# Chained products in PSUM, weight pieces kept from the first half, and operands fetched a stage ahead

## The chip, the cores and the metric

The kernel runs on one core of a Trainium2 chip. The metric is the device time of one execution in microseconds. The median of three runs is 3549.64 us (3546.86 to 3550.24).

## The reference

One layer of an encoder on 2048 tokens of width 1024, fp32: a token mixer (a chunked mLSTM beside an RWKV-7 recurrence), cross-attention on 256 memory rows, and a gated feed-forward part with a causal convolution of width 3; each adds to x behind an RMS norm, and a last norm follows. The part that matters here is the last:

```python
def conv_glu_ffn(h, w_up, conv_w, conv_b, w_down):
    u = h @ w_up
    gate, val = u[..., :D_FF], u[..., D_FF:]
    gate = causal_dwconv(gate, conv_w, conv_b)
    return (jax.nn.silu(gate) * val) @ w_down
...
        h = rmsnorm(x, norm_ffn[l])
        x = x + conv_glu_ffn(h, f_up[l], f_conv_w[l], f_conv_b[l], f_down[l])
    return rmsnorm(x, norm_final)
```

D_FF is 2816, in 22 tiles of 128 (`f` below). The kernel holds everything transposed, features on the partitions and tokens along the free axis.

## The kernel before

Every matmul operand is split into a rounded part hi and a rest lo, and a product is the three matmuls hi·hi, hi·lo and lo·hi, of 128x128 weights against 512 tokens. A split is a cast on ScalarE and a subtraction on VectorE or GpSimd (`resplit`, L1330 and L1331).

The mixer takes the first 1335 us and is not touched. All that follows is one block whose instructions a scheduler has put in order beforehand, engine by engine, by a model of their costs; on the chip each engine works through its queue in that order. SP issues all DMAs, in order too. The block goes over two halves of 1024 tokens; a half has two blocks of 512 (`NB`).

For each half: cross-attention (`attention`, with `out_proj` for the second block, and `attn_out`, which also makes the seven operands that the up-projection needs), then `ffn_up`, then `ffn_down`. The output projection of the next half's first block stands ahead of the last of the four groups of `ffn_down` (`ahead`).

`ffn_up` takes the gate and the value columns of one f as a 2x2 block matrix (input halves against gate and value), and the two token blocks as the other side, and forms the result by seven products instead of eight: weights a11, a12, a22 and the sums s1 to s4 against the operands 11, t1, t3, t2, 21, 22, t4. Each product is 12 matmuls, so 84 per f. The raw columns come by `load_raw` (two buffers, `wraw`); s1 to s4 are added in fp32 (L1417 to L1420) and the seven pieces are split, in both halves anew. Four PSUM tiles X, Z, W, Y take the products; p1, p5 and p7 are copied to SBUF (L1436), and VectorE and GpSimd add them (u2 at L1451, p7+p5 at L1452, c21 at L1479, p7+u2 at L1480). `gate(b)` multiplies by the row scale bc3, runs the convolution (Identity on ScalarE, two taps at L1467), the tanh (L1470), L1471 and a multiplication by bc3 on GpSimd (L1472). L1482 makes the result and L1483 stores it to `act_dram`.

`ffn_down` goes through four groups (token block b, output half dh). Each takes 22 steps of 12 matmuls (L1502 to L1504). A step loads 256 KB of weights into `wdr` (6 buffers, shared with other temporaries) and splits them into `wd`; in groups with dh 0 it loads and splits the activations of that f as well. At a group's end the four sums are added to x2 (L1508), and behind dh 1 the last norm follows.

## Time and profile before

| | us |
|---|---|
| median of three runs | 3549.64 |
| the profiled execution | 3561.95 |
| its span | 3560.2 |
| TensorE busy in it | 3281.8 |
| VectorE busy | 2298.4 |
| GpSimd busy | 1581.8 |
| ScalarE busy | 1355.2 |

The granted TensorE clock is 0.963 over the span. Up-projections lie at 1717 to 2197 us and 2780 to 3269 us, the first down-projection begins at 2216 us (the next half's output projection is in it), the second lies at 3285 to 3544 us. A line of a timeline has the start, the duration, the engine, the line of the program, the operation with output and inputs, its shape, and in brackets how long the engine was idle just before and what released it. Matmuls overlap, so their pace is the distance of their starts. Releasers are inferred.

### The profile page before, as it was taken

Reading aid. Unit: us, or ns where it says so; the run is one execution under the profiler, and the core shown is the slowest. Engines: PE = TensorE matmul, PEld = TensorE weight load, DVE = VectorE, ACT = ScalarE, POOL = GpSimd, SP = SyncE. Lnnn points to the kernel's source line nnn. Section 1 sums busy time; section 2 is a strip of 40 time slices with the busy share of each in tenths; the row PEclk is TensorE's granted clock in tenths of the full one; section 3 lists DMA queues with packets and bytes.
Section 4 is the critical chain, followed back from the end, with each engine's and each line's share of the span. In section 5 each row is a group of like instructions: output and inputs, shape, how many; then the busy total and the mean of one; then the engine's idle time right before and its main releaser. Section 6 shows DMA issues by size and latency. Waiting matters only on the chain. (4 is left out here: it accounts for less than half of the span.)

```text
span 3560.2 us, 48232 instructions
## 1 busy us (share of the span) xinstructions
PE 3281.8 (92%) x16860; PEld 2654.7 (75%) x16860; DVE 2298.4 (65%) x4104; ACT 1355.2 (38%) x2703; POOL 1581.8 (44%) x1486
## 2 busy tenths in 40 slices
PE   6999999999999988999799997997999799997998
PEld 5777778788778777787677775876887677775876
DVE  5787777777777764343798999222233799899221
ACT  5345433533434345332333334333232333334322
POOL 5332121211211123431788887554231688886543
PEclk9999999999999999999899998998999899998999
DMA  6555444544544448657222224444557222223442
GB/s 215 199 176 174 141 141 138 169 130 128 157 127 137 129 151 266 231 173 248 80 74 71 74 72 167 157 158 143 171 172 240 83 76 72 74 74 144 155 151 83
DMA packets 279283, 509.28 MB, mean 143 GB/s; under 512 B 85504, under 2 KB 117376, under 8 KB 279040
## 3 DMA queue, kind: packets, MB, share of 16 engines
q1 hardware_dynamic: 274816, 504.10, 43.1%
q8 instruction: 133, 2.18, 0.3%
q10 hardware_dynamic: 4224, 2.10, 0.2%
q14 instruction: 110, 0.90, 0.1%
HBM read 396.96 MB, written 109.12 MB: 142 GB/s over the span
## 5 line engine op out<-in xcount | busy, mean ns | idle before, releaser
L147 PE MATMUL pd<-hA,whl 128*128 128x512 f32 x2976 | 815.5, 411 | 14.7 <-ACT whl L121 6.6
L147 PEld LDWEIGHTS pd<-hA,whl 128*128 128x128 f32 x2976 | 535.1, 191 | 119.2 <-ACT whl L121 8.3
L1430 PE MATMUL pd<-h,ws 128*128 128x512 f32 x704 | 293.3, 417 | 59.0 <-ACT ws L1330 59.0
L1502 PE MATMUL dps<-act,wd 128*128 128x512 f32 x704 | 281.8, 400 | 66.7 <-ACT wd L1330 66.7
L1331 POOL TENSOR_TENSOR wd<-wdr,wd 128x512 fp32r<-128x512 f32 x176 | 235.6, 1355 | 194.6 <-ACT wd L1330 192.4
L124 POOL TENSOR_TENSOR whl<-wraw,whl 128x512 fp32r<-128x512 f32 x137 | 187.0, 1375 | 253.4 <-ACT whl L121 245.3
L1431 PE MATMUL pd<-h,ws 128*128 128x512 f32 x704 | 284.8, 405 | 0.0
L1503 PE MATMUL dps<-act,wd 128*128 128x512 f32 x704 | 280.7, 399 | 0.0
L1432 PE MATMUL pd<-h,ws 128*128 128x512 f32 x704 | 271.2, 406 | 0.0
L1504 PE MATMUL dps<-act,wd 128*128 128x512 f32 x704 | 268.4, 392 | 1.1 <-POOL wd L1331 1.1
L1430 PEld LDWEIGHTS pd<-h,ws 128*128 128x128 f32 x704 | 137.7, 196 | 117.8 <-ACT ws L1330 94.9
L1331 POOL TENSOR_TENSOR a<-wraw,a 128x512 fp32r<-128x512 f32 x132 | 210.4, 1594 | 2.2 <-ACT a L1330 2.2
L1502 PEld LDWEIGHTS dps<-act,wd 128*128 128x128 f32 x704 | 135.7, 193 | 98.0 <-ACT wd L1330 69.7
L1430 PE MATMUL pd<-h,a 128*128 128x512 f32 x528 | 206.7, 391 | 0.0
L1431 PE MATMUL pd<-h,a 128*128 128x512 f32 x528 | 206.0, 390 | 0.0
L1432 PE MATMUL pd<-h,a 128*128 128x512 f32 x528 | 205.8, 390 | 0.0
L1331 POOL TENSOR_TENSOR ws<-sr,ws 128x512 fp32r<-128x512 f32 x88 | 146.9, 1670 | 88.4 <-ACT ws L1330 88.4
L1219 POOL TENSOR_TENSOR sq<-sq 128x512 f32<-128x512 f32 x56 | 76.0, 1357 | 231.6 <-ACT sq L1216 230.2
L1432 PEld LDWEIGHTS pd<-h,ws 128*128 128x128 f32 x704 | 137.1, 195 | 42.3 <-POOL ws L1331 11.3
L1330 ACT CAST wd<-wdr 128x512 fp32r<-128x512 f32 x176 | 108.2, 619 | 158.4 <-PE dps L1504 101.4
L1472 POOL TENSOR_TENSOR fu<-fu,bcs 128x512 f32<-128x512 f32 x88 | 142.2, 1616 | 54.4 <-DVE fu L1471 54.4
L1508 DVE TENSOR_TENSOR x<-dps,x 128x512 f32<-128x512 f32 x32 | 21.7, 690 | 214.0 <-PE dps L1504 214.0
(992 smaller groups left out, 8054.6 us busy)
## 6 DMA issues: line engine op xcount, KB each, us to landing
whl<-w_split SPq DMA_DIRECT2D x186, 512.0 KB
wraw<-f_up SPq DMA_DIRECT2D x88, 512.0 KB
wdr<-f_down SPq DMA_DIRECT2D x176, 256.0 KB
wqk<-qk_dram SPq DMA_DIRECT2D x64, 512.0 KB
wvo<-vo_dram SPq DMA_DIRECT2D x64, 512.0 KB
w_split<-whl SPq DMA_DIRECT2D x62, 512.0 KB
act_dram<-fu SPq DMA_DIRECT2D x88, 256.0 KB
act<-act_dram SPq DMA_DIRECT2D x88, 256.0 KB
```

The source lines that it names most:

```text
L124: (nc.vector if dve else nc.gpsimd).tensor_tensor(t_[:, 1], r_, t_[:, 0].bitcast(F32), ALU.subtract)
L147: nc.tensor.matmul(out_, lhsT, rhs, **kw)
L1219: (nc.vector if fast else nc.gpsimd).tensor_tensor(acc, acc, sq, ALU.add)
L1330: nc.scalar.copy(t_[:, 0], raw)
L1331: eng.tensor_tensor(t_[:, 1], raw, t_[:, 0].bitcast(F32), ALU.subtract)
L1430: nc.tensor.matmul(ps, w[:, 0, k, :], B[b][k][:, 0, :], start=(k == 0 and not more), stop=False, skip_group_check=True)
L1431: nc.tensor.matmul(ps, w[:, 0, k, :], B[b][k][:, 1, :], start=False, stop=False, skip_group_check=True)
L1432: nc.tensor.matmul(ps, w[:, 1, k, :], B[b][k][:, 0, :], start=False, stop=(k == H - 1), skip_group_check=True)
L1472: nc.gpsimd.tensor_tensor(u, u, bc3[b], ALU.mult)
L1502: nc.tensor.matmul(pss[i], hi[:, i, :], a[:, 0, :], start=(f == 0), stop=False)
L1503: nc.tensor.matmul(pss[i], hi[:, i, :], a[:, 1, :], start=False, stop=False)
L1504: nc.tensor.matmul(pss[i], lo[:, i, :], a[:, 0, :], start=False, stop=(f == NFF - 1))
```

## The change

Four things change, all of them in the second block.

The products are accumulated in PSUM in chains: X takes a11, s2, s3 and a22 in turn and is copied out after each but the last (p1, u2, u3), Z takes s1 and then s4, and R takes a12. There are three PSUM tiles per f, and the additions u2, c21, p7+p5 and p7+u2 are replaced by an addition R+p1 in gate(0) and u3+p5 on GpSimd. gate(0) now adds from PSUM and multiplies by bc3 in SBUF, as gate(1) did. ScalarE copies four tiles per f.

In the first half each split piece is stored to `ws_dram` (512 KB each). The second half loads the seven pieces of an f from there and splits none of them.

The down-projection's operands are fetched ahead: in the last f of `ffn_up` the first four weights and the first seven activations, before each group's drain the first four weights of the next group, and activations of the second block during the group before it. `wdr` moves to another pool of four buffers.

In `attn_out` the sum of squares stands ahead of the splits, for the second block on VectorE; the row scale of the second block is made after the products of f = 0.

```diff
+    ws_dram = dram.tile([NFF, 7, P, 2, KT // 2, P], F32, name="ws_dram")
...
+            acc = sum_sq(acc, x, d, o == 1)
...
-            acc = sum_sq(acc, x, d)
...
+    def up_weights(hf, f):
 
         H = KT // 2
-        whl = lambda name: wpool.tile([P, 2, H, P], FR, tag="whl", name=name, bufs=WB)
-        bc3 = None
+        pcs = {}
+
+        def piece(i, name):
+            pool = name[0] == "a"
+            pcs[name] = wpool.tile([P, 2, H, P], FR, tag="whl", name="wa", bufs=WB) if pool else KQ((P, 2, H, P), "ws")
+            if hf:
+                nc.sync.dma_start(pcs[name].bitcast(F32), ws_dram[f, i])
+            return pcs[name]
...
+        rg, rv = load_raw(t_in["f_up"][f]), load_raw(t_in["f_up"][NFF + f])
+        g1, g2, v1, v2 = rg[:, :H], rg[:, H:], rv[:, :H], rv[:, H:]
+        s1r, s2r, s3r, s4r = [t_[:, u] for t_ in [K4((P, 2, H, P), "sr", F32) for _ in range(2)] for u in range(2)]
+        raws = dict(a11=g1, a12=g2, a22=v2, s1=s1r, s2=s2r, s3=s3r, s4=s4r)
+        for i, name in enumerate(order):
+            t_ = piece(i, name)
+            if name == "s1":
+                nc.gpsimd.tensor_tensor(s1r, v1, v2, ALU.add)
+            elif name == "s2":
+                nc.vector.tensor_tensor(s2r, s1r, g1, ALU.subtract)
+            elif name == "s3":
+                nc.vector.tensor_tensor(s3r, v1, g1, ALU.subtract)
+            elif name == "s4":
+                nc.gpsimd.tensor_tensor(s4r, g2, s2r, ALU.subtract)
+            resplit(t_, nc.vector if name in ("s2", "s3") else nc.gpsimd, raws[name])
+            if S > HALF:
+                nc.sync.dma_start(ws_dram[f, i], t_.bitcast(F32))
+        return pcs
...
+            last = f == NFF - 1
+            X, Z, R = [PD(name="pd") for _ in range(3)]
+            prod(X, "a11", "11")
             p1 = kept(X, "p1")
-            prod(Z, s1, "t1")
+            prod(Z, "s1", "t1")
             p5 = kept(Z, "p5")
-            prod(W, s3, "t3")
-            p7 = kept(W, "p7")
-            prod(Y, s2, "t2")
-            if bc3 is None:
-                norm_bc(st[NB - 1])
-                bc3 = [s_["bc3"] for s_ in st]
-            u2 = T(name="u2")
-            nc.vector.tensor_tensor(u2, Y, p1, ALU.add)
-            nc.gpsimd.tensor_tensor(p7, p7, p5, ALU.add)
+            if last:
+                early(range(3))
+            prod(X, "s2", "t2", True)
+            u2 = kept(X, "u2")
+            prod(R, "a12", "21")
+            if last:
+                early(range(3, 7))
...
-                if b == 0:
-                    nc.vector.tensor_tensor(gt_[:, 2:], X, bc3[b], ALU.mult)
-                else:
-                    nc.vector.tensor_tensor(gt_[:, 2:], Z, u2, ALU.add)
-                    nc.vector.tensor_tensor(gt_[:, 2:], gt_[:, 2:], bc3[b], ALU.mult)
+                nc.vector.tensor_tensor(gt_[:, 2:], (R, Z)[b], (p1, u2)[b], ALU.add)
+                nc.vector.tensor_tensor(gt_[:, 2:], gt_[:, 2:], st[b]["bc3"], ALU.mult)
...
-            prod(X, a12, "21", True)
-            gate(0)
-            prod(Z, s4, "22", True)
+                nc.gpsimd.tensor_tensor(u, u, st[b]["bc3"], ALU.mult)
+
+            if f:
+                gate(0)
+            prod(X, "s3", "t3", True)
+            u3 = kept(X, "u3")
+            nc.gpsimd.tensor_tensor(u3, u3, p5, ALU.add)
+            prod(Z, "s4", "22", True)
+            if f == 0:
+                prod(X, "a22", "t4", True)
+                norm_bc(st[NB - 1])
+                gate(0)
             gate(1)
-            prod(W, a22, "t4", True)
-            nc.vector.tensor_tensor(c21, W, u2, ALU.add)
-            nc.vector.tensor_tensor(p7, p7, u2, ALU.add)
-            for b, c in enumerate((c21, p7)):
+            if f:
+                prod(X, "a22", "t4", True)
+            for b, c in enumerate((X, u3)):
...
+    class Down:
+
+        def __init__(self, hf):
+            self.hf, self.have = hf, {}
+
+        def act(self, b, f):
+            if (b, f) not in self.have:
+                a = self.have[b, f] = K4((P, 2, TB), "act")
+                nc.sync.dma_start(a[:, 1].bitcast(F32), act_dram[self.hf, f, b])
+                resplit(a, nc.vector)
+            return self.have[b, f]
+
+        def w(self, b, dh, f):
+            H = KT // 2
+            if (b, dh, f) not in self.have:
+                w, raw = KQ((P, 2, H, P), "wd"), TQ((P, H, P), "wdr")
+                nc.sync.dma_start(raw, t_in["f_down"][f][:, dh * H:(dh + 1) * H])
+                resplit(w, nc.gpsimd, raw)
+                self.have[b, dh, f] = w
+            return self.have[b, dh, f]
+
+        def early(self, fs):
+            for f in fs:
+                if f < 4:
+                    self.w(0, 0, f)
+                self.act(0, f)
...
+                if dh == 1 and b + 1 < NB and 6 <= f < 12:
+                    D.act(b + 1, f - 6)
...
+            if not lastg:
+                for f in range(4):
+                    D.w(*groups[n + 1], f)
```

VectorE in the up-projection of half 0, before, from the late part of one f to the start of the next (pd is a PSUM tile, sr an unsplit sum, ws a split piece, bcs the row scale, fu the gate):

```order
2743 L1464 TENSOR_TENSOR gt__18790<-gt__18790,bcs_17781 128x512
2744 L1331 TENSOR_TENSOR ws_18828<-sr_18831,ws_18828 128x512
2745 L1331 TENSOR_TENSOR ws_18829<-sr_18832,ws_18829 128x512
2746 L1467 SCALAR_TENSOR_TENSOR fu_18753<-gt__18790,vec_68,fu_18753 128x512 x2
2747 L1479 TENSOR_TENSOR c21_18754<-pd_18694,u2_18750 128x512
2748 L1482 SCALAR_TENSOR_TENSOR fu_18753<-fu_18753,c21_18754 128x512
2749 L1471 SCALAR_TENSOR_TENSOR fu_18753<-fth_18798,fu_18753 128x512
2750 L1482 SCALAR_TENSOR_TENSOR fu_18753<-fu_18753,p7_18736 128x512
2751 L1451 TENSOR_TENSOR u2_18909<-pd_18854,p1_18867 128x512
2752 L1480 TENSOR_TENSOR p7_18895<-p7_18895,u2_18909 128x512
2753 L1461 TENSOR_TENSOR gt__18926<-pd_18851,bcs_17312 128x512
```

L1479, L1451 and L1480 in these rows are the additions that go, and L1461 at the end is gate(0)'s multiplication out of PSUM.

The same queue in the changed program, from the two splits of one f over gate(1) to gate(0) of the next:

```order
2682 L1332 TENSOR_TENSOR ws_18212<-sr_18201,ws_18212 128x512
2683 L1332 TENSOR_TENSOR ws_18221<-sr_18202,ws_18221 128x512
2684 L1474 TENSOR_TENSOR gt__18169<-pd_18073,u2_18115 128x512
2685 L1475 TENSOR_TENSOR gt__18169<-gt__18169,bcs_17828 128x512
2686 L1478 SCALAR_TENSOR_TENSOR fu_18129<-gt__18169,vec_68,fu_18129 128x512 x2
2687 L1482 SCALAR_TENSOR_TENSOR fu_18129<-fth_18177,fu_18129 128x512
2688 L1499 SCALAR_TENSOR_TENSOR fu_18129<-fu_18129,u3_18154 128x512
2689 L1474 TENSOR_TENSOR gt__18293<-pd_18237,p1_18250 128x512
2690 L1475 TENSOR_TENSOR gt__18293<-gt__18293,bcs_17313 128x512
2691 L1430 TENSOR_TENSOR sr_18365<-wraw_18362,wraw_18360 128x512
2692 L1478 SCALAR_TENSOR_TENSOR fu_18292<-gt__18293,vec_68,fu_18292 128x512
2693 L1499 SCALAR_TENSOR_TENSOR fu_18129<-fu_18129,pd_18072 128x512
```

gate(1) now stands as one run, with the final of u3 right behind it, and gate(0) of the next f begins with an addition and a multiplication; the final that reads the PSUM tile (pd) stands between the two taps of the next f.

GpSimd in the changed program at the same f:

```order
626 L1483 TENSOR_TENSOR fu_18129<-fu_18129,bcs_17313 128x512
627 L1332 TENSOR_TENSOR ws_18226<-sr_18202,ws_18226 128x512
628 L1479 COPY fcar_15470<-gt__18169 128x2
629 L1332 TENSOR_TENSOR wa_18366<-wraw_18360,wa_18366 128x512
630 L1473 COPY gt__18293<-fcar_15470 128x2
631 L1483 TENSOR_TENSOR fu_18129<-fu_18129,bcs_17828 128x512
632 L1489 TENSOR_TENSOR u3_18154<-u3_18154,p5_18101 128x512
633 L1332 TENSOR_TENSOR wa_18380<-wraw_18360,wa_18380 128x512
```

The addition of p5 to u3 stands directly behind gate(1)'s multiplication; before, the addition of p7 and p5 stood behind it in the same way, but the row that read it was not the next one of VectorE.

In the second half of the changed program one f has ten such rows on VectorE (four for each gate and two finals); no difference and no split is left.

SP before the last group of half 0, before (wdr are down weights, wraw and x the output projection's operands):

```order
1203 L1262 DMA x_22864<-xT 128x512
1204 L96 DMA wraw_23947<-w_out 128x1024
1205 L1270 DMA x1_dram_15462<-x_22864 128x512
1206 L1262 DMA x_22907<-xT 128x512
1207 L1270 DMA x1_dram_15462<-x_22907 128x512
1208 L1262 DMA x_22950<-xT 128x512
1209 L1270 DMA x1_dram_15462<-x_22950 128x512
1210 L1518 DMA wdr_22990<-f_down 128x512
1211 L1518 DMA wdr_23007<-f_down 128x512
```

Here the weight loads of the last group follow the output projection's last store.

The same place in the changed program:

```order
1361 L1518 DMA wdr_22700<-f_down 128x512
1362 L1518 DMA wdr_23147<-f_down 128x512
1363 L1518 DMA wdr_23164<-f_down 128x512
1364 L1518 DMA wdr_23181<-f_down 128x512
1365 L1518 DMA wdr_23198<-f_down 128x512
1366 L1518 DMA wdr_23215<-f_down 128x512
1367 L1518 DMA wdr_23232<-f_down 128x512
1368 L1263 DMA x_22759<-xT 128x512
1369 L1518 DMA wdr_23249<-f_down 128x512
1370 L1271 DMA x1_dram_15462<-x_22759 128x512
```

Six of the last group's weight loads now stand ahead of the output projection's first load of x and a seventh ahead of its first store; the four before them (the last is row 1361) stand there as well.

## Rows read from the trace of the kernel before

**Rows 1.** Windows of three stretches: busy time by engine, granted clock, DMA share.

```profile
core 0: us, PE busy (x) PEld busy (x) DVE busy (x) ACT busy (x) POOL busy (x), PEclk, DMA share, GB/s
1350.00:1400.00 50.00, 45.92 (x303) 40.28 (x302) 24.65 (x38) 27.85 (x52) 18.76 (x15) 0.97 0.92 294
1745.60:2196.00 450.40, 424.36 (x1779) 334.66 (x1779) 407.15 (x380) 169.76 (x294) 367.88 (x294) 0.98 0.22 75
3269.10:3285.30 16.20, 0.01 (x1) 0.01 (x1) 16.20 (x26) 13.66 (x25) 4.75 (x3) 0.58 1.03 388
```

**Rows 2.** Timeline of TensorE: start, duration, operation, idle before and its releaser.

```profile
1679.48 0.39 PE L176 MATMUL pd<-pt,wvo 128*128 128x512 f32 x1
...
1692.86 0.39 PE L175 MATMUL pd<-pt,wvo 128*128 128x512 f32 x1
...
1717.88 1.87 PE L1225 MATMUL ssps<-ones,sq 128*128 128x1 f32 x8 [10.13 <-POOL sq L1219]
...
2216.36 0.80 PE L1502 MATMUL dps<-act,wd 128*128 128x512 f32 x1 [18.82 <-ACT wd L1330]
...
2476.90 0.80 PE L1502 MATMUL dps<-act,wd 128*128 128x512 f32 x1 [20.93 <-ACT wd L1330]
...
2789.43 1.87 PE L1225 MATMUL ssps<-ones,sq 128*128 128x1 f32 x8 [9.26 <-POOL sq L1219]
...
2796.55 1.86 PE L1234 MATMUL bcB<-ident,rstd 128*128 128x128 f32 x7 [5.25 <-POOL rstd L183]
...
3285.29 0.80 PE L1502 MATMUL dps<-act,wd 128*128 128x512 f32 x1 [16.20 <-ACT wd L1330]
...
3544.11 0.39 PE L1504 MATMUL dps<-act,wd 128*128 128x512 f32 x1
```

**Rows 3.** All operations of line L1461, two of half 0: durations, start.

```profile
L1461 DVE TENSOR_TENSOR gt__17972<-pd,bcs x1: 677/677/677, 1766.6 to 1766.6; 128x512 f32<-128x512 f32 x1
...
L1461 DVE TENSOR_TENSOR gt__20834<-pd,bcs x1: 676/676/676, 2153.8 to 2153.8; 128x512 f32<-128x512 f32 x1
```

**Rows 4.** Timeline of VectorE, one f of the up-projection.

```profile
1895.63 0.68 DVE L1461 TENSOR_TENSOR gt__18926<-pd,bcs 128x512 f32<-128x512 f32 x1
1896.23 0.68 DVE L1418 TENSOR_TENSOR sr<-wraw 128x512 f32<-128x512 f32 x1
1897.26 2.28 DVE L1467 SCALAR_TENSOR_TENSOR fu<-gt__18926,vec,fu 128x512 f32<-128x512 f32 x2 [0.35 <-POOL fcar L1468]
...
1901.26 1.78 DVE L1464 TENSOR_TENSOR gt__18949<-gt__18949,bcs 128x512 f32<-128x512 f32 x1
...
1913.63 1.76 DVE L1482 SCALAR_TENSOR_TENSOR fu<-fu,p 128x512 f32<-128x512 f32 x1 [1.41 <-POOL fu L1472]
1915.31 0.68 DVE L1451 TENSOR_TENSOR u<-pd,p 128x512 f32<-128x512 f32 x1
1916.09 1.14 DVE L1480 TENSOR_TENSOR p<-p,u 128x512 f32<-128x512 f32 x1
1917.15 0.68 DVE L1461 TENSOR_TENSOR gt__19085<-pd,bcs 128x512 f32<-128x512 f32 x1
```

**Rows 5.** Waits of TensorE, 1350 to 3560 us: total, times, longest.

```profile
PE pd L1430 <- ACT ws L1330: 59.0, 42, 2.1
```

**Rows 6.** Timeline of GpSimd in the same f.

```profile
1912.30 1.29 POOL L1472 TENSOR_TENSOR fu<-fu,bcs 128x512 f32<-128x512 f32 x1 [0.63 <-DVE fu L1471]
1913.55 1.29 POOL L1452 TENSOR_TENSOR p<-p,p 128x512 f32<-128x512 f32 x1
```

**Rows 7.** Timeline of VectorE, first f of half 0.

```profile
1744.95 0.69 DVE L1451 TENSOR_TENSOR u<-pd,p 128x512 f32<-128x512 f32 x1 [7.61 <-PE pd L1432]
...
1757.01 2.45 DVE L1467 SCALAR_TENSOR_TENSOR fu<-gt__17836,vec,fu 128x512 f32<-128x512 f32 x2 [0.95 <-ACT fu L1465]
```

**Rows 8.** Waits of TensorE, 2230 to 2470 us.

```profile
PE dps L1502 <- ACT wd L1330: 6.7, 2, 4.7
```

**Rows 9.** DMA issues on SP before the last group of half 0.

```profile
2472.84 0.33 SPq L1270 DMA_DIRECT2D x_dram<-x  x1
2473.22 6.92 SPq L1518 DMA_DIRECT2D wdr<-f_down  x6
```

More of the change, by code (lines that the diff above doesn't have):

```diff
@@ new lines, in up_weights @@
+        pcs = {}
[5 more added lines that the diff above has]
+            return pcs[name]
+        order = ("a11", "s1", "s2", "a12", "s3", "s4", "a22")
+        if hf:
+            for i, name in enumerate(order):
+                piece(i, name)
+            return pcs
@@ new lines, in ffn_down, with step @@
+            lastg = n == len(groups) - 1
+            if dh == 0:
+                xs, acc = [], None
+            if lastg:
+                ahead()
+            tail = 4 if lastg else 0
+            pss = [PD(name="dps") for _ in range(H)]
+            def step(f, i):
+                w, a = D.w(b, dh, f), D.act(b, f)
+                nc.tensor.matmul(pss[i], w[:, 0, i, :], a[:, 0, :], start=(f == 0), stop=False)
+                nc.tensor.matmul(pss[i], w[:, 0, i, :], a[:, 1, :], start=False, stop=False)
+                nc.tensor.matmul(pss[i], w[:, 1, i, :], a[:, 0, :], start=False, stop=(f == NFF - 1))
@@ new lines, in ffn_down @@
+            for f in range(NFF):
+                D.w(b, dh, f)
+                D.act(b, f)
+                if f < NFF - tail:
+                    for i in range(H):
+                        step(f, i)
+                if f in (NFF - 4, NFF - 2):
+                    xx = K4((P, 2, TB), "x2", F32)
+                    for u in range(2):
+                        nc.sync.dma_start(xx[:, u], x2_dram[len(xs), :, ts_])
+                        xs.append(xx[:, u])
+                if dh == 1 and b + 1 < NB and 6 <= f < 12:
+                    D.act(b + 1, f - 6)
@@ new lines, in ffn_down @@
+            if not lastg:
+                for f in range(4):
+                    D.w(*groups[n + 1], f)
+            for i in range(H):
+                for f in range(NFF - tail, NFF):
+                    step(f, i)
+                x = xs[dh * H + i]
+                nc.vector.tensor_tensor(x, pss[i], x, ALU.add)
+                acc = sum_sq(acc, x, dh * H + i, True)
+            if dh:
+                bc = bcast_sbuf(acc)
+                for d in range(KT):
+                    nc.vector.scalar_tensor_tensor(xs[d], xs[d], V("norm_final", d), bc, ALU.mult, ALU.mult)
+                    nc.sync.dma_start(out[d * P:(d + 1) * P, ts_], xs[d])
```

89 lines of the change are left out of this document (15 added, 74 removed).

## Prediction

> **What bounds the kernel now.** I read the windows of the stages first, then the waits of TensorE, then the timeline of one f on VectorE and GpSimd, last TensorE's own rows where it stood still longest. In the windows the reader is to see that the gated up-projection is not a transfer problem: the DMA engines are busy 0.22 of it, while VectorE is busy 407 of 450 us; in another stage they carried 294 GB/s at a share of 0.92, so about 320 GB/s is theirs to give [rows 1]. TensorE is busy too, but its rows are modelled ends; its pace is read from spacing: 60 rows from 1679.48 to 1692.86 are 59 steps, 0.2268 us each [rows 2]. The 84 matmuls of one f would take 19.05 us at that pace. One f takes (2153.8 - 1766.6)/18 = 21.51 us [rows 3]. So 2.46 us per f are lost, 22 times in each half.
>
> Who takes them stands in VectorE's timeline [rows 4]: from one L1461 to the next (1895.63 to 1917.15) it is idle only 0.35 + 1.41 us. It works through its queue in order for 19.76 us and waits in it for 1.76; TensorE's 59.0 us behind "ACT ws" [rows 5] are the same delay seen one step on. Why 18 operations of about 0.60 us (issue to issue beside a source in PSUM, 1895.63 to 1896.23) last 19.76 us is in the same rows: those with both inputs in SBUF take 1.7 to 1.8 us when GpSimd works beside them, while those that read PSUM stay at 0.68. GpSimd has ten large operations per f, 1.25 us each when nothing is beside them (1912.30 to 1913.55 [rows 6]).
>
> The rest of the loss is at seams [rows 2]: TensorE waits 10.13 us for the sum of squares before half 0's first up-product, 18.82 between up and down, 20.93 at the last group behind the next half's output projection; in half 1 9.26 and 5.25, then 16.20.
>
> **The change, part by part.**
>
> *Matmuls.* Their number stays, 84 per f and 12 per step of the down-projection. Chaining sums in PSUM takes nothing from TensorE.
>
> *VectorE in half 0.* Three additions go: u2 (0.60 to the next start, or 0.78 as 1915.31 to 1916.09 has it), c21 (as a PSUM reader 0.60) and p7+u2 (1.06). The final of X reads PSUM instead of SBUF, about 0.3 less. gate(0) had one operation (L1461, 0.60); it now has an addition from PSUM (0.60) and a multiplication in SBUF, 0.60 alone or 1.71 beside GpSimd (1901.26 [rows 4] to the next start). Together -2.6 and +0.6 to +1.7: work falls from 19.76 to between 17.8 and 18.9. But waits grow, since the new order gives less to do between a request and its answer: both of gate(1)'s and half of gate(0)'s wait for the Identity of ScalarE stand open (0.95 as in [rows 7], and 0.33 of it), that for tanh costs about 0.7, and the final of u3 now waits for two GpSimd operations in a row, fu*bc3 and then u3+=p5 behind it: 1.41 as now, plus 1.25, is 2.66. In all 4.6 us. A plain sum gives 22.4 to 23.5 per f. Against it stands that GpSimd moves on during those 2.9 new idle us, and each of its operations that runs then lengthens none of VectorE's. The floor is what cannot overlap: ten operations of GpSimd at 1.25 and 13 of VectorE with both inputs in SBUF at 0.60 are 20.3 us. I take 21.8, near the middle of 20.3 and 23.5 and nearest to the row of now: 21 periods cost 6 us (from 25 gained to 42 lost). ScalarE's fourth copy out of PSUM (0.58 by its kind) lies in its idle time.
>
> The Trainium skill ("SBUF — State Buffer", section "SBUF: two separate sides") says that VectorE with two SBUF inputs and GpSimd share a pair of ports as an exclusive lock: whichever starts first holds it for its whole instruction. The rows of 0.68 against 1.7 to 1.8 agree. By that rule the moved multiplication, no longer read from PSUM, costs up to 1.1 us per f, 23 us over 21 periods, and by the other reading, in which it costs 0.60 whatever stands beside it, 23 us less; 21.8 lies between.
>
> *Stores in half 0.* Seven pieces of 512 KB per f besides two raw loads of 512 and two activation stores of 256: 5.24 MB, at 320 GB/s 16.4 us of 21.8. They are hidden if the queue keeps the loads early enough: on SP the second raw load stands behind the store of s3, which waits for VectorE's subtraction, and by the order some 11 us remain before its first reader. If that cover goes, each f pays what is missing of the 11.
>
> *Seams of half 0.* Attention to up: gate(0) of f=0 needs no bc3 of block 1 and VectorE no longer stands 7.61 us [rows 7] for the product s2·t2: 7.5 gained. The statistics' product keeps its place directly before the broadcast, so its wait stays (bounds 0 to 15). Up to down: the first pieces of the down weights are split early, but TensorE's last products wait for the last gate, whose VectorE steps are queued behind the early splits of activations, and the load of the seventh piece stands on SP behind the last activation store: of 18.82 I count 4 (0 to 15). Between the first groups 6.7 us of waiting [rows 8] are lost, and four weights are ready before the drain: 6. Last group: now SP issues its six weight loads at 2473.22, behind the last store of the output projection, 3.7 us before the first matmul that had waited 20.93 [rows 2, 9]; in the new order eleven weights are loaded and seven split before that projection: 21 (10 to 21). Half 0 in all: 7.5 - 6 + 4 + 6 + 21 = 32.5.
>
> *Half 1.* It loads the seven pieces and splits nothing: VectorE keeps 12 operations per f, GpSimd 3, ScalarE 8. By the prices above VectorE's chain is about 12 × 0.6 plus two rounds through ScalarE of 1.7 plus the GpSimd wait of 2.7, some 14 us, under TensorE's 19.05. Loads are 4.19 MB per f, 13.1 us at 320 GB/s. So TensorE binds. The up-projection now runs from 2789.43 - 9.26 = 2780.2 to 3285.29 - 16.20 = 3269.1, 488.9 us [rows 2]; 1836 matmuls (22×84 less the first product, done before) take 416.4. I leave 5 us for the one round of statistics (the 5.25 of now [rows 2]; 0 to 18): 67.5 gained. If loads or copies held it at the present pace, 52 of it (21 × 2.46) would not come. Up to down: 16.2 falls to about 4.5, the wait for the last activation's store, load and split (0 to 16): 12. Its stretch has the DMA engines at a share of 1.03 [rows 1], so what is fetched early is taken off a full resource. The down-projection lasts 258.8 (3285.29 to 3544.11) for 1056 matmuls, 239.5; I count 5 of the 19 (0 to 12). The tail after 3544.11, 16 us, stays. Half 1: 84.5.
>
> *Sum.* 32.5 + 84.5 = 117. The profiled execution took 3561.95 (span 3560.2), to 3445. The median of the runs is 12.3 lower, 3549.64; the change takes off stalls that both have, so 3432.
>
> **The rivals.**
>
> (a) Half 0 falls to TensorE's pace as well. For it: three VectorE operations less, and half of GpSimd's work could run in VectorE's idle time. Against: the floor of 20.3 us that cannot overlap. At 19.05 plus nothing, the steady term is +51 in place of -6: 3375.
>
> (b) VectorE in half 0 gets slower, the plain sum of 23.5 us: the wait for the two GpSimd operations is in each f and nothing is put between. For it: [rows 4], where one such operation already costs 1.41. Against: less contention. 21 × 1.7 = 36 more: 3468.
>
> (c) Half 1 doesn't speed up: the change doesn't do what it says, since a load can only be issued when its buffer is free and SP's queue also holds the activation stores, which wait for VectorE's finals. Against: each piece's buffer is freed over 16 us before its use. 52 lost: 3484.
>
> (d) Slower than before: moved data. Both halves become a transfer of 5.24 + 4.19 = 9.43 MB per pair of f's, paid at the rate that mixed stores and loads on one ordered queue get. It decides when 22 × (9.43/rate - 21.8 - 19.05) passes 117 us, under 204 GB/s. At 195 it costs 166: 3598. For it: the pieces are both written and read within the same memory, which no stretch of the trace shows together with a rate; against: 294 GB/s over 50 us and 388 over 16 [rows 1].
>
> **How the numbers follow.** Forecast 0.52; (a) 0.12; (b) 0.17; (c) 0.11; (d) 0.08. All but (d) are faster by over 0.2%, which is about what a measurement here can tell from no change. (d) begins at that border: 0.07 slower and 0.01 the same; another 0.01 for the same where (b) and (c) meet with seams that give nothing; 0.91 faster. Range: fast side, half 0 at its floor (-31), transitions at their better ends (-30): 3371, so 3370. Slow side, (b) with half the loss of (c), 36 + 26: 3494. Outside lie (d) and the ends of (a) and (c).
>
> **What would show it.** Starts of gate(0)'s first VectorE operation in half 0: 21.8 us apart (19.1 is (a), 23.5 (b)); in half 1: 19.05 (21.5 is (c)), with TensorE's idle near zero. VectorE's final of u3 shows an idle of about 2.7 behind "POOL u3". The last group of half 0 starts within 1 us of the output projection's end; the one before it is no later. DMA share about 0.75 in half 0's up-projection and 0.65 in half 1's; if it nears 1, (d). I am wrong as a whole if half 1 keeps 21.5, or half 0 passes 27 us per f.

## The result and the profile after

The changed kernel takes 3437.26 us in the median of three runs (3434.74, 3437.26, 3446.18). A fourth run was slow, 4259.97 us at a granted clock of 0.692, and is left out. The kernel before takes 3549.43. The ratio is 0.9691 (95% interval 0.9669 to 0.9713), 110 us less by the ratio and 112 by the medians. The profiled execution took 3434.74, its span is 3433.0, 127.2 shorter than the span before.

First the windows of the two up-projections in the trace after (columns as in [rows 1]):

```profile
core 0: us, PE busy (x) PEld busy (x) DVE busy (x) ACT busy (x) POOL busy (x), PEclk, DMA share, GB/s
1800.00:2150.00 350.00, 321.16 (x1328) 255.06 (x1328) 273.58 (x254) 138.45 (x238) 265.64 (x222) 0.97 0.67 239
2850.00:3100.00 250.00, 250.00 (x1105) 207.07 (x1104) 118.70 (x157) 66.70 (x104) 70.16 (x91) 1.00 0.65 220
```

In half 1 TensorE is busy for the whole of the 250 us at a granted clock of 1.00 (0.97 in this window before); VectorE, which was busy nine tenths of the time there, is down to 119. In half 0 TensorE still has gaps. The DMA engines now work at 0.67 and 0.65 of their time, where it was 0.22.

The first VectorE operation of gate(0), which answers to [rows 3] (line 1474 now), two of half 0 and two of half 1:

```profile
L1474 DVE TENSOR_TENSOR gt__17967<-pd,p x1: 680/680/680, 1751.3 to 1751.3; 128x512 f32<-128x512 f32 x1
...
L1474 DVE TENSOR_TENSOR gt__20901<-pd,p x1: 678/678/678, 2148.6 to 2148.6; 128x512 f32<-128x512 f32 x1
...
L1474 DVE TENSOR_TENSOR gt__25855<-pd,p x1: 693/693/693, 2817.3 to 2817.3; 128x512 f32<-128x512 f32 x1
...
L1474 DVE TENSOR_TENSOR gt__26550<-pd,p x1: 691/691/691, 2912.4 to 2912.4; 128x512 f32<-128x512 f32 x1
```

Half 0: 18 periods in 397.3 us, 22.07 each, where it was 21.51. Half 1: five in 95.1, 19.02 each, the pace of 84 matmuls at [rows 2].

VectorE through one f of half 0, which answers to [rows 4]:

```profile
1905.74 0.68 DVE L1474 TENSOR_TENSOR gt__19108<-pd,p 128x512 f32<-128x512 f32 x1
...
1908.03 1.56 DVE L1478 SCALAR_TENSOR_TENSOR fu<-gt__19108,vec,fu 128x512 f32<-128x512 f32 x1 [0.28 <-ACT fu L1476]
...
1919.63 2.44 DVE L1478 SCALAR_TENSOR_TENSOR fu<-gt__19147,vec,fu 128x512 f32<-128x512 f32 x2 [0.96 <-ACT fu L1476]
1922.78 0.69 DVE L1482 SCALAR_TENSOR_TENSOR fu<-fth,fu 128x512 f32<-128x512 f32 x1 [0.70 <-ACT fth L1481]
1926.12 1.76 DVE L1499 SCALAR_TENSOR_TENSOR fu<-fu,u 128x512 f32<-128x512 f32 x1 [2.66 <-POOL u L1489]
1927.81 0.68 DVE L1474 TENSOR_TENSOR gt__19271<-pd,p 128x512 f32<-128x512 f32 x1
```

Four waits stand in the period: 0.28 and 0.96 for the Identity, 0.70 for the tanh, and 2.66 for GpSimd's addition of p5 to u3. That is 4.60 us of idle time, where it was 1.76; the work fell from 19.76 to 17.47.

TensorE at the seams, which answers to [rows 2]:

```profile
1705.40 1.87 PE L1226 MATMUL ssps<-ones,sq 128*128 128x1 f32 x8 [6.02 <-DVE sq L1220]
...
1709.88 2.07 PE L1235 MATMUL bcB<-ident,rstd 128*128 128x128 f32 x8 [2.61 <-POOL rstd L183]
...
1721.26 0.79 PE L1446 MATMUL pd<-h,ws 128*128 128x512 f32 x1 [9.31 <-ACT ws L1331]
...
2199.22 0.50 PE L1545 MATMUL dps<-act,wd 128*128 128x512 f32 x1 [2.00 <-ACT wd L1331]
...
3162.47 0.39 PE L1545 MATMUL dps<-act,wd 128*128 128x512 f32 x1
```

In half 0 the wait for the sum of squares is 6.02 in place of 10.13, but the split of s1 comes behind it with 9.31. The down-projection's first matmul waits 2.00 in place of 18.82 in half 0, and in half 1 it follows the matmul before it by one step. It is no longer behind the whole up-projection: the scheduler puts the first steps of the down-projection between the last products of the last f (18 matmuls from 2199.22, then a product at 2204.02, and so on), and the last product waits 1.84 us more.

The stages of the two profiled executions, in us, from landmarks in TensorE's rows:

| from, to | before | after | saved | the prediction's term |
|---|---|---|---|---|
| start, first matmul of the second block | 1416.5 | 1409.4 | 7.1 | none (same code) |
| to the end of half 0's attention | 288.2 | 286.9 | 1.3 | none |
| to gate(0) of f = 1 | 62.0 | 55.0 | 6.9 | 7.5 |
| 18 periods of the up-projection | 387.2 | 397.3 | -10.1 | -5 (-6 for 21) |
| to the end of the third group | 259.4 | 249.2 | 10.3 | 4 + 6 |
| output projection, to the last group's first matmul | 63.7 | 43.8 | 19.9 | 21 |
| last group | 67.9 | 66.4 | 1.5 | none |
| half 1: attention | 232.2 | 226.6 | 5.6 | none |
| up- and down-projection | 767.0 | 682.1 | 84.9 | 84.5 |
| tail | 16.1 | 16.4 | -0.3 | 0 |

The landmark of gate(0) stands behind five of the seven products before and behind four after, so up to 2.7 us (12 matmuls) may belong to the fifth row and not to the third.

### The profile page after: what moved, and what is told of

Its sections match the earlier page's. It is cut to its first block, busy times and chain, and to the rows that moved or that the text cites. A ratio compares the mean times of both kernels' runs of the same rounds, so it can differ in the third digit from the quotient of the medians.

```text
span 3433.0 us, 48215 instructions
## 1 busy us (share of the span) xinstructions
PE 3242.5 (94%) x16860; PEld 2646.4 (77%) x16860; DVE 2038.0 (59%) x3942; ACT 1300.0 (38%) x2593; POOL 1283.5 (37%) x1318
## 4 chain that ended last, share of the span: by engine, by line
PE 55%; DVE 15%; DMA 9%; POOL 8%; issue 8%; ACT 4%; SPq 1%; POOLq 0%; DVEq 0%; ACTq 0%
PE pd L147 11%; PE pd L1446 4%; PE pd L1447 4%; PE pd L1448 4%; DMA x<-x_dram 4%; PE dps L1547 3%; PE dps L1545 3%; PE dps L1546 3%; PE qy L147 2%; PE pd L176 2%; PE pd L173 2%; PE pd L175 2%; PE sc L1298 2%; PE sc L1300 2%; PE sc L1299 2%
## 5 line engine op out<-in xcount | busy, mean ns | idle before, releaser
L147 PE MATMUL pd<-hA,whl 128*128 128x512 f32 x2976 | 814.5, 411 | 16.1 <-ACT whl L121 7.8
L1545 PE MATMUL dps<-act,wd 128*128 128x512 f32 x704 | 275.8, 392 | 7.2 <-DVE x L1569 3.8
L1546 PE MATMUL dps<-act,wd 128*128 128x512 f32 x704 | 275.4, 391 | 0.0
L1547 PE MATMUL dps<-act,wd 128*128 128x512 f32 x704 | 270.6, 392 | 4.6 <-POOL wd L1332 4.6
L1446 PE MATMUL pd<-h,wa 128*128 128x512 f32 x528 | 207.3, 396 | 9.6 <-ACT u L1452 9.6
L1447 PE MATMUL pd<-h,wa 128*128 128x512 f32 x528 | 207.1, 392 | 0.0
L1448 PE MATMUL pd<-h,wa 128*128 128x512 f32 x528 | 207.0, 392 | 0.0
L1446 PEld LDWEIGHTS pd<-h,ws 128*128 128x128 f32 x704 | 135.8, 193 | 83.5 <-ACT u L1452 38.0
L1483 POOL TENSOR_TENSOR fu<-fu,bcs 128x512 f32<-128x512 f32 x88 | 132.2, 1502 | 102.3 <-DVE fu L1482 92.2
L1448 PEld LDWEIGHTS pd<-h,ws 128*128 128x128 f32 x704 | 135.8, 193 | 33.2 <-POOL ws L1332 4.6
L1545 PEld LDWEIGHTS dps<-act,wd 128*128 128x128 f32 x704 | 132.9, 189 | 36.2 <-ACT wd L1331 4.3
L1547 PEld LDWEIGHTS dps<-act,wd 128*128 128x128 f32 x704 | 132.5, 189 | 33.8 <-POOL wd L1332 6.3
L1447 PEld LDWEIGHTS pd<-h,ws 128*128 128x128 f32 x704 | 135.9, 193 | 28.5 <-DVE h L1332 0.4
L1546 PEld LDWEIGHTS dps<-act,wd 128*128 128x128 f32 x704 | 133.0, 189 | 27.7
L1332 DVE TENSOR_TENSOR act<-act 128x512 fp32r<-128x512 f32 x88 | 73.7, 860 | 108.7 <-ACT act L1331 107.6
```

Of the source, the lines that this page charges most:

```text
L147: nc.tensor.matmul(out_, lhsT, rhs, **kw)
L1332: eng.tensor_tensor(t_[:, 1], raw, t_[:, 0].bitcast(F32), ALU.subtract)
L1446: nc.tensor.matmul(ps, w[a][:, 0, k, :], B[b][k][:, 0, :], start=(k == 0 and not more), stop=False, skip_group_check=True)
L1447: nc.tensor.matmul(ps, w[a][:, 0, k, :], B[b][k][:, 1, :], start=False, stop=False, skip_group_check=True)
L1448: nc.tensor.matmul(ps, w[a][:, 1, k, :], B[b][k][:, 0, :], start=False, stop=(k == H - 1), skip_group_check=True)
L1483: nc.gpsimd.tensor_tensor(u, u, st[b]["bc3"], ALU.mult)
```

## The experiments

All times below are medians, each beside runs of the kernel before on the same chip (3548 to 3554); the changed kernel itself stands at 3437, ratio 0.9691.

### Half 1 and the stores

**Splitting twice.** No piece is stored or loaded; half 1 loads raw columns and splits.

```diff
-            if hf:
-                nc.sync.dma_start(pcs[name].bitcast(F32), ws_dram[f, i])
...
-            if S > HALF:
-                nc.sync.dma_start(ws_dram[f, i], t_.bitcast(F32))
```

> Edit: the changed kernel without the stored pieces: half 0 stores none, half 1 loads the raw columns and splits them anew. Chains, early operands and the early sum of squares stay. Theory 1 (half 1's gain is the splitting that it is spared, and the stores of half 0 are hidden): half 1 gets half 0's period, 22.07 in place of 19.05, 21 times 3.0 is 63 us, and half 0's waits at the start, some 8 us more; half 0 stays at 22.07. In all about 3508. Rival (the stores cost time in half 0): half 0 falls to 21.5 or less, 3495 or less.

Measured: 3507.6, ratio 0.9876 (0.9851 to 0.9900). gate(0)'s first operation, two of half 0, two of half 1:

```profile
L1465 DVE TENSOR_TENSOR gt__17952<-pd,p x1: 678/678/678, 1751.9 to 1751.9; 128x512 f32<-128x512 f32 x1
...
L1465 DVE TENSOR_TENSOR gt__19200<-pd,p x1: 679/679/679, 1928.5 to 1928.5; 128x512 f32<-128x512 f32 x1
...
L1465 DVE TENSOR_TENSOR gt__25456<-pd,p x1: 677/677/677, 2790.8 to 2790.8; 128x512 f32<-128x512 f32 x1
...
L1465 DVE TENSOR_TENSOR gt__26860<-pd,p x1: 676/676/676, 2989.5 to 2989.5; 128x512 f32<-128x512 f32 x1
```

Eight periods in half 0 take 176.6 us, nine in half 1 198.7: 22.08 in both. Without the stores half 0 is no faster, so they were covered; and half 1's gain is the splitting it is spared. Some 70 us of the 110 hang on the stored pieces (66 by the ratios).

**Three more stores per f.**

```diff
                 nc.sync.dma_start(ws_dram[f, i], t_.bitcast(F32))
+                if i < 3:
+                    nc.sync.dma_start(ws2_dram[f, i], t_.bitcast(F32))
```

> Edit: in half 0 three of the seven pieces of each f are stored a second time to another place, 1.57 MB more per f: 6.81 MB, 308 GB/s at a period of 22.07. Theory 1 (transfers of half 0 are covered, VectorE's queue sets the pace): period 22.07, 3437 within 5 us, the share of the DMA engines rises to nearly 1. Rival (transfers are at the border already, or raw loads behind more stores on SP's queue come late): 6.81 MB at 280 GB/s are 24.3 us, 21 times 2.2 is 47 us: 3484.

Measured: 3452.8, ratio 0.9718 (0.9692 to 0.9744). Half 0 in the window from 1800 to 2150, and two waits of VectorE in it:

```profile
1800.00:2150.00 350.00, 309.48 (x1266) 243.88 (x1266) 258.89 (x245) 131.88 (x228) 256.80 (x215) 0.96 0.78 290
```
```profile
1921.58 0.69 DVE L1477 TENSOR_TENSOR gt__19341<-pd,u 128x512 f32<-128x512 f32 x1 [3.19 <-PE pd L1451]
...
1944.23 0.69 DVE L1477 TENSOR_TENSOR gt__19507<-pd,u 128x512 f32<-128x512 f32 x1 [4.51 <-PE pd L1451]
```

This run doesn't answer its question. With more stores the scheduler put half 0 in another order, in which VectorE waits for TensorE, and the period varies between 17 and 26 us. The rival is not refuted by it either: ScalarE waits 25.0 us for raw loads between 1800 and 2200, eight times, and not once in the changed kernel. It shows only that 290 GB/s were carried at a share of 0.78, so the transfers as such were not at their limit. What settles the stores is the run before.

### The seams

**Nothing fetched ahead.**

```diff
-            if last:
-                early(range(3))
...
-            if last:
-                early(range(3, 7))
...
-                if dh == 1 and b + 1 < NB and 6 <= f < 12:
-                    D.act(b + 1, f - 6)
-            if not lastg:
-                for f in range(4):
-                    D.w(*groups[n + 1], f)
```

> Edit: the changed kernel without any operand fetched ahead for the down-projection: no weights and activations in the last f of the up-projection, no weights ahead of a group's drain, no activations of the second block ahead. Theory 1 (each of these waits is taken off in full): the waits before the down-projection come back, some 13 us in half 0 and 12 in half 1, 20 us before the last group of half 0, some 4 between the other groups: about 3486. Rival (the scheduler, free to put loads early, places some of them ahead anyway since buffers are what limits them): less than half of it comes back, 3460.

Measured: 3444.3, ratio 0.9699 (0.9674 to 0.9725), not told apart from the changed kernel. From the third group's end to the last group's first matmul it takes the same 43.75 us as in the changed kernel. So the lines that fetch ahead are not needed for it, and my theory for this term fell. What is left of the change there is the pool of the raw weights. TensorE's waits for the split of a down weight or an activation, from 2195 us to the end (total, times, longest), in the kernel before:

```profile
PE dps L1502 <- ACT wd L1330: 66.7, 7, 20.9
```

in the changed kernel:

```profile
PE dps L1545 <- ACT wd L1331: 3.4, 2, 2.0
```

and in this one:

```profile
PE dps L1541 <- ACT wd L1331: 7.1, 4, 3.7
```

Of 66.7 us 3.4 are left with the lines and 7.1 without them. At the step from the up- to the down-projection of half 0 the lines take 3.6 us off TensorE's waits (4.1 in place of 7.7), but the last period of the up-projection is 1.65 us longer with them.

**The kernel before with wdr in the other pool.** One word differs from the kernel before:

```diff
-                    w, raw = KQ((P, 2, H, P), "wd"), T((P, H, P), "wdr")
+                    w, raw = KQ((P, 2, H, P), "wd"), TQ((P, H, P), "wdr")
```

> Edit: the kernel BEFORE with one word changed: the raw down weights wdr are taken from the pool TQ (4 buffers) instead of T (6 buffers, which the gate's temporaries and the output projection's x pass through in turn). No early fetching, no chains, no stored pieces. Theory 1 (new, from the run without early fetching: the loads at the seams were late because a buffer of T was given back late, and the scheduler puts loads ahead by itself once they have buffers of their own): most of the waits before the down-projections, 18.8 and 16.2 us, and before the last group of half 0, 20.9, go: some 45 us, 3504. Theory 2 (the prediction's: it takes loads and splits written ahead): the waits stay, 3549 within 5.

Measured: 3490.9 where the kernel before took 3553.6 on the same chip, ratio 0.9826 (0.9811 to 0.9842): 63 us for one word, more than theory 1 had counted. Three of its waits, 2195 us to the end:

```profile
PE pd L1430 <- ACT ws L1330: 28.9, 21, 1.8
PE dps L1502 <- ACT act L1330: 13.5, 2, 7.5
PE dps L1502 <- DVE x L1508: 4.4, 1, 4.4
```

The 66.7 us behind "ACT wd" are gone and 13.5 behind "ACT act" and 4.4 behind a drain have come, 49 us less; the up-projection's waits (L1430) stay. The waits for sums of squares (L1225) fall as well, from 21.7 to 14.9, and 1.1 behind "POOL wd" goes. Of the other 6 us a part is the granted clock. Behind such a stop in the kernel before it was 0.50, the lower of its two levels, 1.2 and 2.4 GHz (columns as in [rows 1]; the clock is the third from the end):

```profile
2216.00:2220.00 4.00, 3.64 (x8) 2.51 (x8) 2.83 (x6) 1.54 (x3) 4.00 (x2) 0.50 1.05 411
```

and the matmuls start 0.43 us apart (2216.95 to 2217.38) in place of 0.227. I have not followed the rest.

From the third group's end to the last group's first matmul this run too takes 43.75 us, where the kernel before took 63.70. SP's issues of the last group's weight loads show why (x10 are ten in a row):

```profile
2365.02 23.56 SPq L1518 DMA_DIRECT2D wdr<-f_down  x10
...
2391.37 0.33 SPq L1518 DMA_DIRECT2D wdr<-f_down  x1
```

Eleven of the 22 are issued before the output projection's first store, as in the changed kernel, and nothing in the program was written ahead; in the kernel before all came behind its last store [rows 9].

**The changed kernel with wdr back in T.**

```diff
-                w, raw = KQ((P, 2, H, P), "wd"), TQ((P, H, P), "wdr")
+                w, raw = KQ((P, 2, H, P), "wd"), T((P, H, P), "wdr")
```

> Edit: the changed kernel with wdr back in the pool T, the fetching ahead as written in the change. Theory 1 (the pool decides): the waits at the seams come back, up to 45 us: 3470 to 3480. Rival (each of the two suffices: what is written ahead gets its buffers in the turn in which it is written): under 10 us come back, 3437 to 3447.

Measured: 3436.1, ratio 0.9674 (0.9658 to 0.9689): no different from the changed kernel. 15.1 us of waits behind "ACT wd" are there, 11.0 of them in one stop at 2464 us, in the last group of half 0; the other 52 are not:

```profile
PE dps L1545 <- ACT wd L1331: 15.1, 3, 11.0
```

SP's issues for that group:

```profile
2371.55 5.81 SPq L1518 DMA_DIRECT2D wdr<-f_down  x4
...
2460.68 0.92 SPq L1518 DMA_DIRECT2D wdr<-f_down  x2
```

The four weights that the program writes ahead are loaded ahead, the fifth follows the output projection, and TensorE stops for it 48 matmuls (four steps) into the group. With the other pool eleven are ahead. So for the last group the pool is enough by itself, in the kernel before too. That fetching ahead is enough without it is not shown: at the last group it leaves 11.0 us, and elsewhere the other parts of the change were there as well (u2 and c21 have left T); a changed kernel with neither was not run. Why a load in T comes late I read from the code alone: a wdr takes its turn in T behind temporaries of the gate or x tiles that are still in use.

**The sum of squares as before.**

```diff
-            acc = sum_sq(acc, x, d, o == 1)
...
+            acc = sum_sq(acc, x, d)
             if d == 0:
```

> Edit: the changed kernel with the sum of squares of the attention's output where it was before, behind the splits and on GpSimd. Theory 1 (the earlier sum takes off the wait for the statistics at each half's start): the waits of 10.13 and 9.26 us come back, less what the split of s1, which is the next wait of half 0 (9.31), hides of it: 8 to 12 us more, about 3447. Rival (the waits at the start have the s1 split behind them, which is late anyway): within 3 us of 3437.

Measured: 3444.1, ratio 0.9692 (0.9671 to 0.9713), not told apart from the changed kernel. The interval reaches 7.5 us to either side, so the time alone does not exclude the lower end of theory 1. The trace speaks for the rival: the 10.13 and 9.26 do not come back, the waits there are 2.32 and 2.28 us, and at the start of half 0 the statistics and the split of s1 together cost TensorE 14.0 us of waits, where it is 17.9 in the changed kernel. Nothing that this part gains could be measured.

### Half 0

**Without the chains.** The products, copies and additions of the up-projection as in the kernel before, everything else as changed.

```diff
-            prod(X, "s2", "t2", True)
-            u2 = kept(X, "u2")
+            prod(Y, "s2", "t2")
+            u2 = T(name="u2")
+            nc.vector.tensor_tensor(u2, Y, p1, ALU.add)
+            nc.gpsimd.tensor_tensor(p7, p7, p5, ALU.add)
...
```

> Edit: the products of the up-projection as in the kernel before (four PSUM tiles, u2, c21 and p7+u2 added on VectorE, p7+p5 on GpSimd), all else as in the changed kernel: stored and loaded pieces, operands fetched early, sum of squares early. Theory 1 (the chaining takes 2 us of work from VectorE but puts 2.9 us of waits in its order, so in half 0 it costs 0.56 us per f): half 0 falls back to 21.5, 12 us faster there; in half 1 VectorE has 15 operations, some 16 us in 19.05, so TensorE still sets the pace: 3425 in all. Rival (half 1 needs the chaining, since the additions bind VectorE): half 1 rises over 19.05, at 20.5 by 30 us: 3455. Second rival: the stores make half 0 slower, then it stays at 22.07 without the chains and the time at 3437.

Measured: 3428.4, ratio 0.9652 (0.9634 to 0.9669), 9 us under the changed kernel by the medians, 14 by the ratios (the intervals only touch). gate(0)'s first operation in half 0 and in half 1:

```profile
L1481 DVE TENSOR_TENSOR gt__17987<-pd,bcs x1: 678/678/678, 1758.2 to 1758.2; 128x512 f32<-128x512 f32 x1
...
L1481 DVE TENSOR_TENSOR gt__21141<-pd,bcs x1: 678/678/678, 2166.3 to 2166.3; 128x512 f32<-128x512 f32 x1
...
L1481 DVE TENSOR_TENSOR gt__25805<-pd,bcs x1: 692/692/692, 2799.4 to 2799.4; 128x512 f32<-128x512 f32 x1
...
L1481 DVE TENSOR_TENSOR gt__28361<-pd,bcs x1: 691/691/691, 3142.1 to 3142.1; 128x512 f32<-128x512 f32 x1
```

19 periods of 21.48 in half 0, 18 of 19.04 in half 1. The chaining costs 0.59 us per f in half 0, 12 us in all, and gives the pace of half 1 nothing.

**Five divisions of the work between VectorE and GpSimd.** First, bc3 multiplies u3 + p5 and no longer the gate, so that nothing of GpSimd lies behind the gate:

```diff
-                nc.gpsimd.tensor_tensor(u, u, st[b]["bc3"], ALU.mult)
+                v = (u, u3)[b]
+                nc.gpsimd.tensor_tensor(v, v, st[b]["bc3"], ALU.mult)
```

> Edit: gate(1) no longer multiplies the gate by bc3 on GpSimd; GpSimd multiplies u3 + p5 by bc3 instead, which does not depend on the gate, so no GpSimd operation stands between VectorE's L1482 and its final any more. Number of operations on every engine unchanged. Theory 1 (VectorE's queue in order sets half 0, and the 2.67 us wait for two GpSimd operations is in its path): the wait falls to about 1.2 us, since GpSimd can begin the two only behind the piece that it splits at that time; the period of one f falls from 22.07 to about 20.6, 21 periods give 31 us: about 3406. Theory 2 (VectorE and GpSimd together, 20.3 us of operations that cannot overlap, already set the pace and the wait only shows it): the operations are the same, so the period stays within 0.4 of 22.07, 3430 to 3441. Half 1 stays at 19.05 by both.

Measured: 3430.6, ratio 0.9659 (0.9644 to 0.9674), period 21.97 (nine in 197.7 us). The wait hardly moved. ScalarE, GpSimd and VectorE there, in three fences:

```profile
1940.02 0.63 ACT L1481 ACTIVATE fth<-fu 128x512 f32<-128x512 f32 x1 [2.09 <-DVE fu L1478]
1940.56 0.57 ACT L1452 COPY u<-pd 128x512 f32<-128x512 f32 x1
```

```profile
1941.20 1.32 POOL L1491 TENSOR_TENSOR u<-u,p 128x512 f32<-128x512 f32 x1 [1.18 <-ACT u L1452]
```

```profile
1943.92 1.76 DVE L1501 SCALAR_TENSOR_TENSOR fu<-fu,u 128x512 f32<-128x512 f32 x1 [2.55 <-POOL u L1484]
```

ScalarE's copy of u3 out of PSUM (1940.56) stands in its queue behind the tanh of gate(1), which waits for VectorE's taps. GpSimd waits 1.18 for the copy, then adds and multiplies, and VectorE waits 2.55. What I took for free of the gate by its data still depended on it by ScalarE's order. So the run has theory 2's time without testing either theory.

Second, u3 + p5 on VectorE:

```diff
-            nc.gpsimd.tensor_tensor(u3, u3, p5, ALU.add)
+            nc.vector.tensor_tensor(u3, u3, p5, ALU.add)
```

> Edit: u3 + p5 is added on VectorE instead of GpSimd, in both halves. VectorE gets one operation more (0.60 to 1.7 us), GpSimd one less. Theory 1 (waits in VectorE's order): the final then waits for one GpSimd operation instead of two, and the addition runs inside that wait: period from 22.07 to about 20.9 in half 0, 24 us: about 3413. Theory 2 (VectorE's work sets the period, so more work is a longer period): 22.7 or more, 3450. Half 1 unchanged by both.

Measured: 3415.8, ratio 0.9614 (0.9599 to 0.9629), period 21.21 (eight in 169.7).

```profile
1937.16 0.68 DVE L1489 TENSOR_TENSOR u<-u,p 128x512 f32<-128x512 f32 x1
1939.04 1.76 DVE L1499 SCALAR_TENSOR_TENSOR fu<-fu,u 128x512 f32<-128x512 f32 x1 [1.19 <-POOL fu L1483]
1940.72 0.68 DVE L1474 TENSOR_TENSOR gt__19434<-pd,p 128x512 f32<-128x512 f32 x1
```

The addition (L1489, 0.68) runs while GpSimd multiplies the gate, and the wait falls from 2.66 to 1.19. More work on the engine that sets the pace, and a shorter period. Two readings of it are left: a wait shorter by 1.47 for an operation of 0.68, or 1.25 less and 0.60 more of what the two engines cannot overlap, 0.65 of the 0.86 that came off. That sum alone does not set the period, since it also falls with the chaining (14 VectorE operations with both inputs in SBUF become 13: 20.9 to 20.3), and there the period grew from 21.48 to 22.07.

Third, in half 0 gate(1)'s multiplication on VectorE too:

```diff
-                nc.gpsimd.tensor_tensor(u, u, st[b]["bc3"], ALU.mult)
+                (nc.vector if b and hf == 0 else nc.gpsimd).tensor_tensor(u, u, st[b]["bc3"], ALU.mult)
```

> Edit: as the one before, and in half 0 gate(1)'s multiplication by bc3 is on VectorE as well, so that nothing of GpSimd stands in gate(1) at all: VectorE 18 operations per f, GpSimd 8 large ones. Theory 1: 2.67 us of waiting go, two operations of 0.60 to 1.7 come: period between 20.6 and 22.8, likeliest 20.9; about 3413. Theory 2 (what VectorE and GpSimd cannot overlap sets the pace): GpSimd's eight at 1.25 and VectorE's fifteen at 0.60 are 19.0 in place of 20.3, so the period falls by 1.3 at most, as far as 20.8. Rival: VectorE is simply busy, 22.07 + 1.2 = 23.3, 3463.

Measured: 3404.7, ratio 0.9583 (0.9569 to 0.9597), period 20.83 (eight in 166.6): as expected, but by both theories (20.9 and 20.8), so it doesn't part them.

```profile
1934.95 0.69 DVE L1482 SCALAR_TENSOR_TENSOR fu<-fth,fu 128x512 f32<-128x512 f32 x1 [0.70 <-ACT fth L1481]
1935.67 0.69 DVE L1483 TENSOR_TENSOR fu<-fu,bcs 128x512 f32<-128x512 f32 x1
1936.28 0.68 DVE L1489 TENSOR_TENSOR u<-u,p 128x512 f32<-128x512 f32 x1
1937.00 1.80 DVE L1499 SCALAR_TENSOR_TENSOR fu<-fu,u 128x512 f32<-128x512 f32 x1
```

No wait is left behind the tanh; the two operations (L1483, L1489) take 0.6 to 0.7 us each from start to start, and GpSimd has nothing to do just then (it is idle from 1934.29 to 1936.96).

Fourth, as the third with s2 = s1 - g1 moved to GpSimd:

```diff
-                nc.vector.tensor_tensor(s2r, s1r, g1, ALU.subtract)
+                nc.gpsimd.tensor_tensor(s2r, s1r, g1, ALU.subtract)
```

> Edit: gate(1)'s multiplication and the addition u3 + p5 on VectorE in half 0, and in exchange the subtraction s2 = s1 - g1 on GpSimd, which was idle 6.5 us of the 20.83 of a period there. Theory 1 (VectorE's queue in order still sets half 0): 1.7 us per f less on VectorE (the subtraction stood beside GpSimd): 20.83 falls to between 19.2 and 20.0, likeliest 19.7; 21 times 1.1 is 24 us less than the 3405 without this exchange: about 3381. Rival (what the two engines can't overlap sets it, now 9 of GpSimd at 1.25 and 14 of VectorE at 0.60, 19.65, with GpSimd's chain s1, s2, split, s4, split late for TensorE): no gain, 3405 or over.

Measured: 3406.5, ratio 0.9581 (0.9551 to 0.9611), the rival: no gain over the third.

```profile
1927.76 1.77 DVE L1489 TENSOR_TENSOR u<-u,p 128x512 f32<-128x512 f32 x1
...
1932.66 1.67 DVE L1483 TENSOR_TENSOR fu<-fu,bcs 128x512 f32<-128x512 f32 x1
...
1934.36 1.67 DVE L1499 SCALAR_TENSOR_TENSOR fu<-fu,u 128x512 f32<-128x512 f32 x1
```

L1483 is 1.67 us long here where it was 0.69, and L1489 1.77 where it was 0.68 (L1499 was long before): VectorE has one operation less, and two of its others last 1.0 to 1.1 us longer with GpSimd at work beside them. The period is 20.62.

Last, the final product of gate(1) on GpSimd:

```diff
+                if b:
+                    nc.gpsimd.tensor_tensor(us[:, b], us[:, b], c, ALU.mult)
+                else:
+                    nc.vector.scalar_tensor_tensor(us[:, b], us[:, b], 0.5, c, ALU.mult, ALU.mult)
```

> Edit: the final product of gate(1) with u3 is made on GpSimd, behind the two operations for which VectorE had waited; the factor 0.5 goes into ScalarE's copies of p5 and u3. VectorE loses one operation (1.7) and the wait of 2.67 us, GpSimd gets one (1.25). Theory 1 (VectorE's order alone sets half 0): 22.07 less 4.4 is 17.7, so TensorE's 19.05 or GpSimd's own queue sets it: 19.1 to 19.6, 55 us: 3382. Theory 2 (what cannot overlap: GpSimd 11 operations at 1.25 and VectorE 12 at 0.60, 20.95): 21.0 to 21.8, as the run with s2 on GpSimd came out 0.95 over its sum of 19.65: 3410 to 3430.

Measured: 3405.1, ratio 0.9583 (0.9562 to 0.9604). Eight periods take 165.5 us, 20.69 each, but the first of them is a short one; the rest go at 20.77. GpSimd there:

```profile
1930.54 1.31 POOL L1486 TENSOR_TENSOR fu<-fu,bcs 128x512 f32<-128x512 f32 x1 [1.43 <-DVE fu L1485]
1931.80 1.74 POOL L1492 TENSOR_TENSOR u<-u,p 128x512 f32<-128x512 f32 x1
1933.62 1.62 POOL L1503 TENSOR_TENSOR fu<-fu,u 128x512 f32<-128x512 f32 x1
```

VectorE has lost its longest wait and an operation, and the period is hardly shorter than in the third: GpSimd is idle only 1.43 us of it, and its large operations last 1.3 to 1.75, so its own queue is nearly full. Theory 1 in its plain form (VectorE's order alone) fails here by over a microsecond; the second theory's sum, 20.95, is a little high.

## Why the prediction was right

The forecast, 3432 and 117 us less, met 3437 and 110; what it named for the pace of the two up-projections is in the trace. The five stages for which it had a term other than 0 gave 111.9 us in the two profiled executions, where the terms come to 118. Part of that is luck: within two of the stages errors took each other off.

*Half 1* came as worked out, 84.9 us for 84.5: TensorE sets the pace at 19.02 to 19.04, and the run that splits twice puts it back to 22.08 and 3507.6, where 3508 was expected. Two sizes inside are off. Up to the down-projection's first matmul 74.9 us came for 79.5 (67.5 and 12): the statistics, for which 5 were left, cost TensorE no wait, but at the start it waits 5.4 for the split of an operand ("ACT h") and 2.5 for copies. Behind that matmul 10.0 came for 5. Rival (c) is refuted by the window, rival (d) by half 0's period with and without the stores (22.07, 22.08).

*VectorE in half 0.* The 4.6 us of idle time are the 4.60 in the rows, and the wait for two GpSimd operations is 2.66, as reckoned. The work was 17.47, under my 17.8 to 18.9, I take it since GpSimd moved ahead in the new idle time, but by less than I gave it: 22.07 in place of 21.8, so 0.3 us came off the least plain sum of 22.4 and not 0.6. The term is -12 for 21 periods in place of -6, between the forecast and rival (b). That the chaining is a loss was in the sum's sign, and the run without it shows it by itself.

*The seams of half 0* are right as a sum and wrong in their cause. I gave 21 us to the loads that the change writes ahead of the output projection; 19.9 came, but the run without those lines has the same 43.75 us there. The step that failed is "in the new order eleven weights are loaded and seven split before that projection" as an effect of fetching ahead: the order had it, but the move of wdr to another pool was enough for it, an edit for which I had no term. In the kernel before that one word is worth 63 us. The stage before it, 10.3 for 4 + 6, is right by luck. TensorE's waits from up to down fell from 18.8 to 4.1, far more than the 4; the last two periods of the up-projection, with the early loads and splits in them, are 2.8 us longer; and between the first groups, where 6 were to go, 6.3 us of waits are left of 6.7, 3.8 of them for a drain.

*The start of half 0.* 6.9 us came where 7.5 was forecast, and by its mechanism: VectorE's wait of 7.61 before the first gate(0) is 0.23 after. The sum of squares has no part that can be measured in it: the run with the old place of it is at 3444 with an interval that holds the changed kernel's ratio. The statistics' wait, which was to stay, fell from 10.13 to 6.02, and the split of s1 took its place with 9.31.

*Not in the sum.* The profiled executions differ by 7.1 us before the change's first instruction, and by 5.6 in half 1's attention, 4.5 of it a wait for a sum of squares (5.6 to 1.0); the medians, with 110 in place of 127, don't have all of that.

*VectorE beside GpSimd.* The row of 0.69 for L1483 alone and 1.67 beside GpSimd agree with the Trainium skill ("SBUF — State Buffer", section "SBUF: two separate sides"), which has the two engines share a pair of ports as an exclusive lock. By it, work moved from one of the two to the other buys little by itself: the fourth run of half 0 moved one operation to GpSimd, and the period fell by 0.2 us. My floor from it, operations times 1.25 and 0.60, was not a floor: 20.77 was measured where it gave 20.95, and the other four of these runs ended 1.0 to 1.8 over theirs. What sets half 0's period in full stays open; the runs show that neither VectorE's order alone nor this sum alone does.

The third, the fourth and the last run of half 0, 3404.7 to 3406.5, are the best and can't be told apart: ratios 0.9581 to 0.9583 against the changed kernel's 0.9691, with intervals that don't touch it. A kernel without the chains and with one of those edits was not run.
